# Two of the weight sums of a fast matrix product move from VectorE to accumulating DMAs, and fewer tiles are computed the classical way

## The chip, the core and the metric

The program runs on one core of one Trainium2 chip. The metric is the device time of one execution in microseconds (us), from the first to the last instruction of the core and the little that lies around it. Three runs of the kernel before gave 2911.69, 2925.96 and 2928.84 us; their median is 2925.96 us.

## The reference, cut to what matters

Two transformer blocks over 512 tokens of width 1024, all in float32. Around the change stand five feed-forward layers. Four of them (two in each of the two layers of the first block) are a gated product, the fifth has a convolution of width 3 over the tokens between the product and the gate:

```python
def swiglu(x, w_in, w_out):
    gate, up = jnp.split(x @ w_in, 2, axis=-1)
    return (jax.nn.silu(gate) * up) @ w_out

def conv_ffn(h, w_up, conv_w, conv_b, w_down):
    u = h @ w_up
    u = conv3(u, conv_w) + conv_b
    gate, val = u[..., :2816], u[..., 2816:]
    return (gelu(gate) * val) @ w_down
```

`x @ w_in` is 512 x 1024 by 1024 x 5632: 22 tiles of 128 columns for the gate and 22 for the other half ("up"). The convolution and its bias act on each column of `u` by itself.

## The kernel before

Every float32 matrix is split into a rounded part and a rest (`split`: ScalarE rounds to `h`, VectorE forms `l = src - h`), and every product is three matmuls (`mm3`, lines 292 to 294): h by h, h by the other's l, l by the other's h. The third needs the rest of the weights, `wl`.

An ffn (`ffn` for the four gated ones, the phase `ffn2` for the one with the convolution) works in pairs: pair m is gate tile m and up tile 22 + m, whose weights are 128 x 1024 each. There are 22 pairs. A pair is computed in one of two ways:

- classical: each tile is 8 blocks of 128 rows by two halves of 256 tokens, three matmuls each (`proj_t_steps` at the start of an ffn, `tile_t` in between). That is 96 matmuls of 256 columns for a pair.
- fast (`fast_weights`, `fast_pair`): the pair of tiles, the two halves of the 1024 rows and the two halves of the tokens are a 2 x 2 by 2 x 2 block product, done with 7 products instead of 8. A product is 4 blocks by three matmuls, 12 matmuls of 256 columns; the pair is 84. `fast_weights` makes the seven weight operands: the two halves of w1 (`r1`), two sums in the tile `s`, two in the tile `z`, and the second half of w2 (in `r2`). Four sums of 128 x 512 are made by VectorE (lines 449, 450, 453, 454), then each operand is split. `fast_pair` runs the products 0 to 6 in order and adds their results on ScalarE and VectorE. Products 0 and 1 take r1, 2 and 3 take s, 4 and 5 take z, 6 takes r2.

The token operands of the products 2, 3, 4 and 6 are sums and splits too: `fast_parts` makes them, two steps of four subtractions and three splits on VectorE (tiles `two`, `ts`), at the start of an ffn, when the last tokens have been normalised and transposed.

`FIRST` (2) classical pairs start each ffn, from m = 0, and lie beside `fast_parts`. In the four gated ffns the other 20 pairs are fast. In ffn2 every third pair after that is classical (6 of 20), since VectorE has the convolution there: two multiply-adds of 128 x 511 for a gate tile and two for an up tile (lines 1595, 1596), and the product of the two halves (line 1608).

The helper `ahead` writes the code of `fast_weights` of pair m + 1 behind the products of pair m and before the rest of pair m (silu, or convolution and gate). A scheduler then orders the instructions of each engine; the orders shown below are its result. Every engine runs its own list in order. Loads go out on SyncE's queue (SP). GpSimd (POOL) does only inverse square roots, some loads of gains and a few operations of the token mixing. The buffers concerned: three for raw weights (`wr`), three of each split part (`ws`), seven shared ones of 4 KB per partition (`t4`), which hold s, z, `two`, and in ffn2 `top` and `low`, the results of a fast pair.

Of the kernel before, what the change touches and what calls it, by code (L numbers as in the profile page):

```python
# [9 lines left out]
F32 = mybir.dt.float32  # L10
# [3 lines left out]
AF = mybir.ActivationFunctionType  # L14
ALU = mybir.AluOpType
# [3 lines left out]
S, D, DFF, DEPTH = 512, 1024, 2816, 2  # L19
NT, P = 4, 128  # L20
# [159 lines left out]


LAG, EARLY, OTHERS, DELTA, SLIDING, MLSTM = 24, 1, 2, 1, 1.3, 1
FIRST = 2


class Kernel:
# [192 lines left out]
    def fast_parts(self, pool, ps, keep=False):  # L379


        nc = self.nc
        self.load_late()
        part = lambda x, q, a: x[:, 4 * q:4 * q + 4, 256 * a:256 * a + 256]
        both = lambda q, a: (part(self.xh, q, a), part(self.xl, q, a))
        raw = self.raw
        room = lambda i: pool.tile([P, 1088], F32R, tag=f"T{i}", name="ts")[:, 48:1072].rearrange(
            "p (k n) -> p k n", k=4)
        ts = [[room(2 * i + j) for j in range(2)] for i in range(3)]
        for t, (p0, p1) in enumerate(ps):  # L390
            cs = slice(t * P, (t + 1) * P)
            r0, r1 = raw[0][:, :, cs], raw[1][:, :, cs]
            two = self.t4.tile([P, 2, 4, P], F32, tag="t4", name="two")
            nc.vector.tensor_sub(two[:, 0], p0, r0)
            nc.vector.tensor_sub(two[:, 1], p1, two[:, 0])
            nc.vector.tensor_sub(r0, two[:, 1], r0)
            nc.vector.tensor_sub(r1, r1, two[:, 1])
# [32 lines left out]
    def fast_weights(self, w1, w2):  # L430


        nc = self.nc
        r1, r2 = [self.wr.tile([P, 2, 4, P], F32, tag="raw", name="raw") for _ in range(2)]
        for r, w in ((r1, w1), (r2, w2)):
            nc.sync.dma_start(r.rearrange("p a k n -> p (a k n)"), w.rearrange("p k n -> p (k n)"))
        sub = nc.vector.tensor_sub
        ws = []

        def block(src):  # L440
            h = self.ws.tile(list(src.shape), F32R, tag="wh", name="wh")
            l = self.ws.tile(list(src.shape), F32R, tag="wl", name="wl")
            for i in range(src.shape[1]):
                nc.scalar.copy(h[:, i], src[:, i])  # L444
                ws.append((h[:, i], l[:, i]))
            sub(l, src, h.bitcast(F32))  # L446
        block(r1)
        s = self.t4.tile([P, 2, 4, P], F32, tag="t4", name="s")
        nc.vector.tensor_add(s[:, 1], r2[:, 0], r2[:, 1])
        sub(s[:, 0], s[:, 1], r1[:, 0])  # L450
        block(s)
        z = self.t4.tile([P, 2, 4, P], F32, tag="t4", name="z")
        sub(z[:, 0], r1[:, 0], r2[:, 0])
        sub(z[:, 1], r1[:, 1], s[:, 0])
        block(z)
        block(r2[:, 1:2])
        return ws

    def fast_pair(self, ws, xb, top, low):
# [12 lines left out]
        a, b = slice(0, 256), slice(256, 512)  # L472
        prod(0, x, start=True)
        nc.scalar.copy(top[:, a], x)  # L474
        prod(1, y, start=True)
        nc.vector.tensor_add(top[:, a], y, top[:, a])
        prod(2, x)
        nc.scalar.copy(top[:, b], x)
        prod(3, z, start=True)
        nc.scalar.copy(low[:, b], z)  # L480
        prod(4, x)
        nc.scalar.copy(low[:, a], x)
        nc.vector.tensor_add(low[:, b], low[:, a], low[:, b])
# [155 lines left out]
    def ffn(self, l, f):  # L639
        nc, io = self.nc, self.io  # L640
        base = 8 * l + (0 if f == 1 else 4)
        with self.phase(f"ffn{l}{f}") as pool:
# [5 lines left out]
            w = io[f"f{f}i{l}"]  # L648
# [17 lines left out]
            def products(m, ws):  # L666
                G, low = g[m // 2][:, m % 2], self.t2.tile([P, S], F32, tag="t2", name="low")
                X = self.fast_pair(ws, xb, G, low)

                def rest():  # L670
                    nc.scalar.activation(G, G, AF.Silu)
                    nc.vector.tensor_mul(G[:, 0:256], X, G[:, 0:256])
                    nc.vector.tensor_mul(G[:, 256:512], low[:, 256:512], G[:, 256:512])
                return rest
            self.ahead([(lambda m=m: self.fast_weights(w[m], w[KF + m]), lambda ws, m=m: products(m, ws))
                        for m in range(FIRST, KF)])
# [668 lines left out]
    def block2(self):  # L1345
# [237 lines left out]
            self.proj_n8(lhs, io["w2o"], KD, self.add_x8, [b1, b2, b3, b0], room)  # L1583

        with self.phase("ffn2") as pool:
            cv = pool.tile([P, 4, 56], F32, name="cv")
            nc.sync.dma_start(cv[:, :, 0:44], io["cv2"].rearrange("p (j m) -> p j m", j=4))
            pairs = self.ffn_banks()
# [4 lines left out]
            def conv(c, p, m):  # L1593
                A.activation(c, p, AF.Identity, scale=cv[:, 1, m:m + 1], bias=cv[:, 3, m:m + 1])
                V.scalar_tensor_tensor(c[:, 1:], p[:, 0:S - 1], cv[:, 0, m:m + 1], c[:, 1:], ALU.mult, ALU.add)
                V.scalar_tensor_tensor(c[:, 0:S - 1], p[:, 1:], cv[:, 2, m:m + 1], c[:, 0:S - 1], ALU.mult, ALU.add)

            def gate(m):
                def take(p):
# [1 line left out]
                    A.activation(gm(m), gm(m), AF.Gelu_apprx_tanh)  # L1601
                return take

            def up(m):
                def take(p):
                    c = self.t2.tile([P, S], F32, tag="t2", name="cup")
                    conv(c, p, 22 + m)
                    V.tensor_mul(gm(m), c, gm(m))
                return take
            tiles = []  # L1610
            for m in range(KF):
# [3 lines left out]

            def products(m, ws):
                top, low = [self.t4.tile([P, S], F32, tag="t4", name=n) for n in ("top", "low")]
                X = self.fast_pair(ws, xb, top, low)
                A.copy(low[:, 0:256], X)

                def rest():
                    gate(m)(top)
                    up(m)(low)
                return rest
            todo = []
            for m in range(FIRST, KF):
                if (m - FIRST) % 3 == 2:
                    todo += [(lambda n=n: self.load_t(tiles[n][0]),
                              lambda w, n=n: self.tile_t(xs, w, tiles[n][1])) for n in (2 * m, 2 * m + 1)]
                else:  # L1630
# [38 lines left out]
```

## Time and profile before

| | |
|---|---|
| runs shown | 2911.69, 2925.96, 2928.84 us, median 2925.96 |
| the profiled execution | 2919.21 us |
| its span | 2917.4 us |
| PE busy | 2853.4 us, 98% |
| DVE busy | 1952.8 us, 67% |
| ACT busy | 1425.8 us, 49% |
| POOL busy | 141.6 us, 5% |
| moved by DMA | 250.94 MB, of it 10.90 MB on POOL's queue |

PE is TensorE, DVE VectorE, ACT ScalarE. The profile is of one execution, so durations and waits are taken from its trace, and a sum of them stands beside its 2919.21 us. The end of a matmul is modelled: one of 256 columns is shown as 276 ns, while the next starts after 113 ns. What a stretch of matmuls costs is therefore read from the starts, not from the busy time. The same holds on DVE: a subtraction of 128 x 512 is shown as 0.68 us and the next starts 0.60 us after it.

### The profile page before, as it was taken

What the parts mean: (1) busy time and instruction counts of PE and PEld (TensorE: products, weight loads), DVE (VectorE), ACT (ScalarE), POOL (GpSimd) and SP (SyncE); (2) the same over time, 40 slices, a digit from 0 to 9 for tenths busy, and PEclk for the clock granted to TensorE, in tenths of its full rate; (3) what the DMA queues carried; (4) which work ended last, traced back from release to release, by engine and by line L of the source; (5) the groups of instructions that cost most, each with busy time, mean ns of one, the idle gap of its engine ahead of it and who ended that gap; (6) DMA issues with size and microseconds to landing.
All of it is one profiled execution on the core that took longest, in us unless ns stands there. A gap on an engine that the chain in (4) does not pass through costs nothing. (4 is left out here: it accounts for less than half of the span.)

```text
span 2917.4 us, 47905 instructions
## 1 busy us (share of the span) xinstructions
PE 2853.4 (98%) x19288; PEld 2525.3 (87%) x19288; DVE 1952.8 (67%) x3464; ACT 1425.8 (49%) x2784; POOL 141.6 (5%) x169
## 2 busy tenths in 40 slices
PE   7999999999999999999999999999999999999999
PEld 7998888877999878999887887899987877799987
DVE  7884555756888357887345666788635766689853
ACT  5663443343666345555334343466535456566641
POOL 0000000101000000000000000100000220000000
PEclk9999999999999999999999999999999999999999
DMA  4333322002233333333322001233342210313332
GB/s 154 110 123 109 96 82 65 8 3 71 94 110 116 109 101 94 102 109 112 120 68 85 24 8 37 73 110 110 120 134 81 94 44 1 95 60 109 102 102 93
DMA packets 74542, 250.94 MB, mean 86 GB/s; under 512 B 8624, under 2 KB 10800, under 8 KB 74064
## 3 DMA queue, kind: packets, MB, share of 16 engines
q1 hardware_dynamic: 71376, 236.99, 26.0%
q0 software_dynamic: 2944, 10.90, 1.1%
q8 instruction: 151, 2.47, 0.3%
q14 instruction: 71, 0.58, 0.1%
HBM read 245.76 MB, written 2.10 MB: 85 GB/s over the span
## 5 line engine op out<-in xcount | busy, mean ns | idle before, releaser
L281 DVE TENSOR_TENSOR wl<-raw,wh 128x1024 fp32r<-128x1024 f32 (+2 forms) x218 | 259.2, 1193 | 398.5 <-ACT wh L280 396.6
L280 ACT CAST wh<-raw 128x1024 fp32r<-128x1024 f32 (+2 forms) x218 | 223.7, 1027 | 457.8 <-PE psone L294 303.3
L292 PE MATMUL psfast<-xh,wh 128*128 128x256 f32 x1448 | 402.5, 278 | 0.0
L294 PE MATMUL psfast<-xh,wl 128*128 128x256 f32 x1448 | 401.4, 277 | 0.0
L293 PE MATMUL psfast<-xl,wh 128*128 128x256 f32 x1448 | 401.4, 277 | 0.0
L292 PE MATMUL psfast<-ts,wh 128*128 128x256 f32 x1184 | 328.7, 278 | 0.5
L293 PE MATMUL psfast<-ts,wh 128*128 128x256 f32 x1184 | 328.0, 277 | 0.0
L294 PE MATMUL psfast<-ts,wl 128*128 128x256 f32 x1184 | 328.0, 277 | 0.0
L293 PE MATMUL psone<-wl,gs 128*128 128x512 f32 x720 | 281.0, 390 | 0.0
L294 PE MATMUL psone<-wh,gs 128*128 128x512 f32 x720 | 280.2, 389 | 0.0
L292 PE MATMUL psone<-wh,gs 128*128 128x512 f32 x720 | 278.4, 389 | 0.0
L293 PEld LDWEIGHTS psfast<-xl,wh 128*128 128x128 f32 x1448 | 273.2, 189 | 0.2
L292 PEld LDWEIGHTS psfast<-xh,wh 128*128 128x128 f32 x1448 | 271.9, 188 | 1.4
L294 PEld LDWEIGHTS psfast<-xh,wl 128*128 128x128 f32 x1448 | 271.8, 188 | 0.0
L444 ACT CAST wh<-raw 128x512 fp32r<-128x512 f32 x282 | 175.1, 622 | 153.1 <-PE psfast L293 150.5
L292 PEld LDWEIGHTS psfast<-ts,wh 128*128 128x128 f32 x1184 | 222.4, 188 | 1.5 <-ACT top L474 1.5
L293 PEld LDWEIGHTS psfast<-ts,wh 128*128 128x128 f32 x1184 | 223.3, 189 | 0.0
L292 PE MATMUL psmm<-xh,wh 128*128 128x256 f32 (+1 forms) x712 | 222.1, 314 | 0.6 <-ACT xh L280 0.4
L294 PEld LDWEIGHTS psfast<-ts,wl 128*128 128x128 f32 x1184 | 222.3, 188 | 0.0
L293 PE MATMUL psmm<-xl,wh 128*128 128x256 f32 (+1 forms) x712 | 220.9, 311 | 0.0
L294 PE MATMUL psmm<-xh,wl 128*128 128x256 f32 (+1 forms) x712 | 219.6, 309 | 0.0
L446 DVE TENSOR_TENSOR wl<-raw,wh 128x1024 fp32r<-128x1024 f32 (+1 forms) x188 | 179.0, 952 | 59.0 <-PE psfast L294 36.5
(545 smaller groups left out, 6512.0 us busy)
## 6 DMA issues: line engine op xcount, KB each, us to landing
raw<-f1i SPq DMA_DIRECT2D x88, 512.0 KB, 3.5
raw<-f2i SPq DMA_DIRECT2D x88, 512.0 KB, 3.5
raw<-f1o SPq DMA_DIRECT2D x44, 512.0 KB, 3.8
raw<-f2o SPq DMA_DIRECT2D x44, 512.0 KB, 3.9
raw<-w2u SPq DMA_DIRECT2D x44, 512.0 KB, 3.5
raw<-w2d SPq DMA_DIRECT2D x22, 512.0 KB, 3.7
gain<-gains POOLq DMA_DIRECT2D x19, 512.0 KB, 4.1
raw<-wr SPq DMA_DIRECT2D x16, 512.0 KB, 4.1
```

The lines of the kernel that those rows point to most:

```text
L280: self.rounded = self.nc.scalar.copy(h, src)
L281: self.nc.vector.tensor_sub(l, src, h.bitcast(F32))
L292: mm(out, a[0], b[0], start=start, stop=False, **kw)
L293: mm(out, a[0], b[1], start=False, stop=False, **kw)
L294: mm(out, a[1], b[0], start=False, stop=stop, **kw)
L444: nc.scalar.copy(h[:, i], src[:, i])
L446: sub(l, src, h.bitcast(F32))
```

## The change

Four things, in one step.

1. Two of the four weight sums are made by DMA. The second half of w2 and the first half of w1 are added to a loaded half of w2 by two accumulating DMAs, issued by POOL; SP loads that half of w2 twice more, into s and z. A DMA can add but not subtract, so signs move: all that belongs to the second row of the block product comes out negated, and the multiplication that follows it negates again (a `scalar_tensor_tensor` by -1.0 in the gated ffns, negated convolution weights `minus` in ffn2). VectorE keeps two sums for each pair.
2. `FIRST` becomes 1: one classical pair at the start of each ffn instead of two.
3. In ffn2 every fifth pair after that is classical instead of every third: 4 of 21 instead of 6 of 20.
4. In ffn2 two operations of a fast pair go from VectorE to POOL: the addition to `low` in `fast_pair` (`adder`, line 485 after), and the product of the two halves (line 1612 after).

```diff
-FIRST = 2
+FIRST = 1
...
     def fast_weights(self, w1, w2):
...
         r1, r2 = [self.wr.tile([P, 2, 4, P], F32, tag="raw", name="raw") for _ in range(2)]
-        for r, w in ((r1, w1), (r2, w2)):
-            nc.sync.dma_start(r.rearrange("p a k n -> p (a k n)"), w.rearrange("p k n -> p (k n)"))
+        s, z = [self.t4.tile([P, 2, 4, P], F32, tag="t4", name=n) for n in "sz"]
+        nc.sync.dma_start(flat(s[:, 1]), part(w2, 0))
+        nc.sync.dma_start(flat(z[:, 0]), part(w2, 0))
+        nc.sync.dma_start(r1.rearrange("p a k n -> p (a k n)"), flat(w1))
+        nc.sync.dma_start(flat(r2[:, 1]), part(w2, 1))
+        nc.gpsimd.dma_start(flat(s[:, 1]), part(w2, 1), accum_op=ALU.add)
+        nc.gpsimd.dma_start(flat(z[:, 0]), part(w1, 0), accum_op=ALU.add)
...
         block(r1)
-        s = self.t4.tile([P, 2, 4, P], F32, tag="t4", name="s")
-        nc.vector.tensor_add(s[:, 1], r2[:, 0], r2[:, 1])
-        sub(s[:, 0], s[:, 1], r1[:, 0])
+        nc.vector.tensor_add(s[:, 0], s[:, 1], r1[:, 0])
         block(s)
-        z = self.t4.tile([P, 2, 4, P], F32, tag="t4", name="z")
-        sub(z[:, 0], r1[:, 0], r2[:, 0])
-        sub(z[:, 1], r1[:, 1], s[:, 0])
+        nc.vector.tensor_add(z[:, 1], r1[:, 1], s[:, 0])
         block(z)
         block(r2[:, 1:2])
...
-        nc.vector.tensor_add(low[:, b], low[:, a], low[:, b])
+        (adder or nc.vector).tensor_tensor(low[:, b], low[:, a], low[:, b], ALU.add)
...
-                    nc.vector.tensor_mul(G[:, 0:256], X, G[:, 0:256])
-                    nc.vector.tensor_mul(G[:, 256:512], low[:, 256:512], G[:, 256:512])
+                    for p, h in ((X, G[:, 0:256]), (low[:, 256:512], G[:, 256:512])):
+                        nc.vector.scalar_tensor_tensor(h, p, -1.0, h, ALU.mult, ALU.mult)
...
-            def up(m):
+            def up(m, *cv_):
                 def take(p):
                     c = self.t2.tile([P, S], F32, tag="t2", name="cup")
-                    conv(c, p, 22 + m)
-                    V.tensor_mul(gm(m), c, gm(m))
+                    conv(c, p, 22 + m, *cv_)
+                    (G if cv_ else V).tensor_tensor(gm(m), c, gm(m), ALU.mult)
                 return take
...
-                X = self.fast_pair(ws, xb, top, low)
+                X = self.fast_pair(ws, xb, top, low, G)
...
-                    up(m)(low)
+                    up(m, minus)(low)
...
-                if (m - FIRST) % 3 == 2:
+                if (m - FIRST) % 5 == 4:
```

`fast_parts` has its four subtractions turned in sign to fit (lines 394 to 397 before, 394 and 396 after); their number and size are the same. Line numbers after: 438 to 441 are the loads, 442 and 443 the accumulating DMAs, 454 and 456 the two sums that are left (s and z), 452 the rest parts, 485 the addition to `low`, 487 the second addition to `top`, 1599 and 1600 the convolution, 1612 the product, 659 the product of the classical up tile.

In ffn2, from one fast pair to the next, this stood on VectorE (the rows run from the first-half weights of the next pair, `wl<-raw`, to those of its s and z; `top`, `low` and `cup` belong to the pair that ends):

```order
L446 TENSOR_TENSOR wl<-raw,wh 128x1024
L483 TENSOR_TENSOR low<-low 128x256
L485 TENSOR_TENSOR top<-psfast,top 128x256
L450 TENSOR_TENSOR s<-s,raw 128x512
L454 TENSOR_TENSOR z<-raw,s 128x512
L1595 SCALAR_TENSOR_TENSOR g<-top,cv,g 128x511
L446 TENSOR_TENSOR wl<-s,wh 128x1024
L446 TENSOR_TENSOR wl<-z,wh 128x1024
```

and this stands there now:

```order
L452 TENSOR_TENSOR wl<-raw,wh 128x1024
L487 TENSOR_TENSOR top<-psfast,top 128x256
L1599 SCALAR_TENSOR_TENSOR g<-top,cv,g 128x511
L1600 SCALAR_TENSOR_TENSOR g<-top,cv,g 128x511
L1599 SCALAR_TENSOR_TENSOR cup<-low,minus,cup 128x511
L454 TENSOR_TENSOR s<-s,raw 128x512
L1600 SCALAR_TENSOR_TENSOR cup<-low,minus,cup 128x511
L456 TENSOR_TENSOR z<-raw,s 128x512
L452 TENSOR_TENSOR wl<-s,wh 128x1024
L452 TENSOR_TENSOR wl<-z,wh 128x1024
```

Three multiply-adds of the convolution now stand ahead of the sum s of the next pair and a fourth ahead of z; before, one of them stood behind both.

On POOL in ffn2 nothing stood before. Now, from one fast pair to the next, there is this (`g<-cup,g` is the product of the pair before, `low<-low` the addition of the present pair, and the two DMAs are the accumulations for the pair that follows it):

```order
L1612 TENSOR_TENSOR g<-cup,g 128x512
L485 TENSOR_TENSOR low<-low 128x256
L442 DMA s<-w2u 128x512
L443 DMA z<-w2u 128x512
L1612 TENSOR_TENSOR g<-cup,g 128x512
```

The accumulations for a pair stand behind the addition to `low` of the pair before it.

At the start of the second ffn VectorE now has, from the last steps of `fast_parts` to the first weights of s (`g<-psmm,g` is the product of the one classical up tile, `xl<-raw` belongs to the token operand of product 5):

```order
L394 TENSOR_TENSOR two<-raw,pstr 128x512
L452 TENSOR_TENSOR wl<-raw,wh 128x1024
L396 SCALAR_TENSOR_TENSOR two<-two,pstr 128x512
L396 SCALAR_TENSOR_TENSOR raw<-two,raw 128x4x128
L396 SCALAR_TENSOR_TENSOR raw<-two,raw 128x4x128
L659 TENSOR_TENSOR g<-psmm,g 128x512
L281 TENSOR_TENSOR ts<-two,ts 128x4x128 x2
L281 TENSOR_TENSOR ts<-raw,ts 128x4x128
L454 TENSOR_TENSOR s<-s,raw 128x512
L281 TENSOR_TENSOR xl<-raw,xh 128x4x256
L452 TENSOR_TENSOR wl<-s,wh 128x1024
```

The order is much as it was; what has moved is the matmuls beside it: two classical pairs before, one now.

## Rows read from the trace of the kernel before

**Rows 1.** The page, part 1: busy us, share of the span, instructions of each engine.
```profile
PE 2853.4 (98%) x19288; PEld 2525.3 (87%) x19288; DVE 1952.8 (67%) x3464; ACT 1425.8 (49%) x2784; POOL 141.6 (5%) x169
```

**Rows 2.** Windows: stretch, its us, then PE, PEld, DVE, ACT, POOL busy (instructions), clock, DMA.
```profile
762.80:953.40 190.60, 190.60 (x1681) 190.42 (x1681) 165.17 (x260) 119.05 (x243) 0.57 (x1) 1.00 0.35 114
1167.20:1365.10 197.90, 197.90 (x1681) 197.78 (x1680) 165.14 (x259) 119.21 (x243) 0.57 (x1) 1.00 0.34 108
2589.10:2792.80 203.70, 203.22 (x1755) 201.42 (x1754) 183.53 (x262) 129.12 (x241) 0.00 (x0) 1.00 0.33 104
```

**Rows 3.** Tile psmm on PE in one classical pair of ffn2: durations ns, first and last start.
```profile
L294 PE MATMUL psmm<-xh,wl x32: 276/276/276, 2609.4 to 2619.9; 128*128 128x256 f32 x32
```

**Rows 4.** Tile psmm on PE at the start of each ffn: last start is the end.
```profile
L294 PE MATMUL psmm<-xh,wl x56: 276/276/562, 22.6 to 44.5; 128*128 128x256 f32 x48, 128*128 128x512 f32 x8
L294 PE MATMUL psmm<-xh,wl x56: 276/276/415, 738.9 to 762.6; 128*128 128x256 f32 x48, 128*128 128x512 f32 x8
L294 PE MATMUL psmm<-xh,wl x56: 276/281/398, 1143.2 to 1167.0; 128*128 128x256 f32 x48, 128*128 128x512 f32 x8
L294 PE MATMUL psmm<-xh,wl x56: 276/281/415, 1868.9 to 1893.0; 128*128 128x256 f32 x48, 128*128 128x512 f32 x8
L294 PE MATMUL psmm<-xh,wl x56: 276/281/415, 2565.3 to 2589.0; 128*128 128x256 f32 x48, 128*128 128x512 f32 x8
```

**Rows 5.** Timeline of DVE at the start of the second ffn: start, us, instruction.
```profile
743.15 1.22 DVE L281 TENSOR_TENSOR wl<-raw,wh 128x1024 fp32r<-128x1024 f32 x1
...
747.54 1.29 DVE L281 TENSOR_TENSOR xl<-pstr,xh 128x512 fp32r<-128x512 f32 x2
...
758.29 1.21 DVE L446 TENSOR_TENSOR wl<-raw,wh 128x1024 fp32r<-128x1024 f32 x1
759.43 0.68 DVE L450 TENSOR_TENSOR s<-s,raw 128x512 f32<-128x512 f32 x1
760.03 0.68 DVE L453 TENSOR_TENSOR z<-raw 128x512 f32<-128x512 f32 x1
...
761.24 1.21 DVE L446 TENSOR_TENSOR wl<-s,wh 128x1024 fp32r<-128x1024 f32 x1
```

**Rows 6.** Timelines of DVE: the last token's splits in the first, third and fifth ffn.
```profile
21.88 2.48 DVE L281 TENSOR_TENSOR xl<-pstr,xh 128x512 fp32r<-128x512 f32 x4
...
1152.43 1.28 DVE L281 TENSOR_TENSOR xl<-pstr,xh 128x512 fp32r<-128x512 f32 x2
...
2569.51 1.29 DVE L281 TENSOR_TENSOR xl<-pstr,xh 128x512 fp32r<-128x512 f32 x2 [0.21 <-ACT xh L280]
```

**Rows 7.** Timelines of PE, DVE and ACT in ffn2, one fast pair and its end.
```profile
2620.02 0.28 PE L292 MATMUL psfast<-xh,wh 128*128 128x256 f32 x1
...
2627.04 1.22 DVE L446 TENSOR_TENSOR wl<-raw,wh 128x1024 fp32r<-128x1024 f32 x1 [0.38 <-ACT wh L444]
...
2628.51 0.42 DVE L485 TENSOR_TENSOR top<-psfast,top 128x256 f32<-128x256 f32 x1
...
2630.17 0.74 DVE L1595 SCALAR_TENSOR_TENSOR g<-top,cv,g 128x511 f32<-128x511 f32 x1
2630.83 1.22 DVE L446 TENSOR_TENSOR wl<-s,wh 128x1024 fp32r<-128x1024 f32 x1
...
2627.02 0.37 ACT L482 COPY low<-psfast 128x256 f32<-128x256 f32 x1
...
2628.97 0.82 ACT L1594 ACTIVATE g<-top,cv 128x512 f32<-128x512 f32 x1
```

**Rows 8.** Groups by line on POOL (busy us, mean ns, idle before), and the page's DMA issues.
```profile
L276 POOL TENSOR_TENSOR xr<-xrs,mhalf 128x1 f32<-128x1 f32 x40 | 24.5, 614 | 134.4 <-DVE xrs L275 134.2
L258 POOL DMA_DIRECT2D gain<-gains x19 | 11.2, 589 | 766.3 <-DVE wl L446 739.8 <-PE psD L1310 24.0 <-PE psmm L1507 1.9
L931 POOL TENSOR_TENSOR reg<-reg,consts 128x512 f32<-128x512 f32 x8 | 10.2, 1271 | 2.4 <-DVE reg L928 2.4
...
gain<-gains POOLq DMA_DIRECT2D x19, 512.0 KB, 4.1
```

**Rows 9.** Timeline of POOL in the second ffn's start.
```profile
743.32 1.46 POOL L276 TENSOR_TENSOR xr<-xrs,mhalf 128x1 f32<-128x1 f32 x1 [2.25 <-DVE xrs L275]
```

More of the change, by code (lines that the diff above doesn't have):

```diff
@@ L393, in fast_parts @@
             two = self.t4.tile([P, 2, 4, P], F32, tag="t4", name="two")
[L394 to L397, printed above, removed]
+            nc.vector.tensor_sub(two[:, 0], r0, p0)
+            for out, a, b in ((two[:, 1], two[:, 0], p1), (r0, two[:, 1], r0), (r1, two[:, 1], r1)):
+                nc.vector.scalar_tensor_tensor(out, a, -1.0, b, ALU.mult, ALU.subtract)
             for (h, l), src in zip(ts, (two[:, 0], two[:, 1], r0)):
@@ L433, in fast_weights @@
         nc = self.nc
+        flat = lambda z: z.rearrange("p k n -> p (k n)")
+        part = lambda w, q: flat(w[:, 4 * q:4 * q + 4])
         r1, r2 = [self.wr.tile([P, 2, 4, P], F32, tag="raw", name="raw") for _ in range(2)]
-        for r, w in ((r1, w1), (r2, w2)):
-            nc.sync.dma_start(r.rearrange("p a k n -> p (a k n)"), w.rearrange("p k n -> p (k n)"))
-        sub = nc.vector.tensor_sub
+        s, z = [self.t4.tile([P, 2, 4, P], F32, tag="t4", name=n) for n in "sz"]
[5 more added lines that the diff above has]
+        nc.gpsimd.dma_start(flat(z[:, 0]), part(w1, 0), accum_op=ALU.add)
         ws = []
@@ L445, in block @@
                 ws.append((h[:, i], l[:, i]))
-            sub(l, src, h.bitcast(F32))
+            nc.vector.tensor_sub(l, src, h.bitcast(F32))
         block(r1)
-        s = self.t4.tile([P, 2, 4, P], F32, tag="t4", name="s")
-        nc.vector.tensor_add(s[:, 1], r2[:, 0], r2[:, 1])
-        sub(s[:, 0], s[:, 1], r1[:, 0])
+        nc.vector.tensor_add(s[:, 0], s[:, 1], r1[:, 0])
         block(s)
-        z = self.t4.tile([P, 2, 4, P], F32, tag="t4", name="z")
-        sub(z[:, 0], r1[:, 0], r2[:, 0])
-        sub(z[:, 1], r1[:, 1], s[:, 0])
+        nc.vector.tensor_add(z[:, 1], r1[:, 1], s[:, 0])
         block(z)
@@ L457, in fast_weights, with fast_pair @@
         return ws
-    def fast_pair(self, ws, xb, top, low):
+    def fast_pair(self, ws, xb, top, low, adder=None):
         nc = self.nc
@@ L1585, in block2 @@
         with self.phase("ffn2") as pool:
-            cv = pool.tile([P, 4, 56], F32, name="cv")
+            cv = pool.tile([P, 4, 48], F32, name="cv")
             nc.sync.dma_start(cv[:, :, 0:44], io["cv2"].rearrange("p (j m) -> p j m", j=4))
+            minus = pool.tile([P, 4, 56], F32, name="minus")
+            V.tensor_scalar(minus[:, 0:3, 0:44], cv[:, 0:3, 0:44], -1.0, None, ALU.mult)
             pairs = self.ffn_banks()
@@ L1591, in block2, with conv @@
             gm = lambda m: g[m // 2][:, m % 2]
[L1593 to L1596, printed above, removed]
+            def conv(c, p, m, cv_=cv):
+                A.activation(c, p, AF.Identity, scale=cv_[:, 1, m:m + 1], bias=cv[:, 3, m:m + 1])
+                V.scalar_tensor_tensor(c[:, 1:], p[:, 0:S - 1], cv_[:, 0, m:m + 1], c[:, 1:], ALU.mult, ALU.add)
+                V.scalar_tensor_tensor(c[:, 0:S - 1], p[:, 1:], cv_[:, 2, m:m + 1], c[:, 0:S - 1], ALU.mult, ALU.add)
             def gate(m):
```

## The prediction, made before the result

> **What bounds the kernel now.** I read the page first. PE is busy for 98% of the span and no other engine for more than 67% [rows 1], so the kernel is bound by matmuls, as an average. Since busy PE is modelled, I then took the windows of the stretches that the change touches. Twenty fast pairs of the second ffn are 1680 matmuls in 190.6 us [rows 2]: 0.1135 us each, 9.53 us a pair, with nothing idle between them. DVE is busy 165 of those 190.6 us (instructions that overlap are counted once), so it keeps up without much slack. The third ffn has the same instructions and takes 197.9 us; the clock column says 1.00 there too, so I take those 7.3 us as scatter of this execution, which the change can't be held to. In ffn2, 14 fast and 6 classical pairs take 203.7 us [rows 2]. A classical pair there has 32 groups of three matmuls, the first and the last 10.5 us apart [rows 3]: 0.339 us a group, 10.85 us a pair. 14 x 9.53 + 6 x 10.85 = 198.5, so about 5 us of ffn2 are small waits.
>
> The gain that can be had from the matmuls is thus small: a fast pair is 1.3 us shorter than a classical one. What decides is whether a pair's weights are ready when PE comes to them. For that I read the timelines of DVE, ACT and POOL at the start of an ffn and inside ffn2.
>
> **Part 1: fewer classical pairs.** One pair in each ffn and two more in ffn2 change kind: 5 + 2 = 7 pairs x 1.32 = 9.2 us less PE work.
>
> **Part 2: the sums by DMA, gated ffns.** DVE loses two steps of 0.60 us for each pair (the pitch of rows 759.43 and 760.03 in [rows 5]). PE has no wait there to lose [rows 2], so this is worth 0 beyond the start. Two accumulations a pair land on POOL's queue, which is otherwise empty there; the buffers let s and z run some three pairs ahead, about 28 us, against 4.1 us for a load on that queue [rows 8]. I cost them at 0. If that cover is gone, every pair pays (a rival).
>
> **Part 3: the start of an ffn.** Before, two classical pairs (21.7 us of matmuls) lay beside the last token's splits, `fast_parts` and the first weights. Now one does. I count DVE's list forward from the last token's splits, at 0.60 us for 128 x 512 and 1.14 us for 128 x 1024 (758.29 to 759.43 in [rows 5]). Second ffn: those splits end at about 749.0 (in the trace 747.54 + 1.2; one step of `fast_parts` now stands ahead of them). Up to the end of `wl<-s` come 12 steps of 0.60 and 3 of 1.14: 749.0 + 7.2 + 3.4 = 759.6. PE has done its classical pair by about 752.5 and products 0 and 1 (2.7 us) by 755.4; product 2 needs `wl<-s` at its third matmul, so it starts at 759.4. Five products of 1.36 us later, at 766.2, pairs 0 and 1 are done. Before, they were done at 762.7 [rows 4]. So this start is 3.5 us longer, the saved matmuls included. The fourth ffn has the same order: 3.5.
>
> The same count elsewhere: the first ffn from 24.3 [rows 6]: 15 short and 4 long steps (one of them the second classical tile's weights) end at 37.9, with ACT's hand-overs some 38.5; done at 45.1 against 44.6 [rows 4], +0.6. The third ffn from 1153.6 [rows 6]: 10 short, one addition of 0.34 and 2 long steps, 1162.2; with 1.41 us a product there (197.9 / 140) done at 1169.1 against 1167.1, +2.0. ffn2 from 2570.7 [rows 6]: 15 short, 3 multiply-adds of 0.66 and 2 long ones give 2584.0; done at 2590.6 against 2589.1, +1.5. Sum of the five starts: +11.1 us. Bounds: if all of it hides, 5 x -1.3 = -6.6; if the first accumulation is late as well, some 4 us more each, +30.
>
> **Part 4: from one fast pair to the next in ffn2.** After the change m = 1 to 4, 6 to 9, 11 to 14, 16 to 19 and 21 are fast: 12 places where a fast pair follows a fast one. Take T = the start of product 5; in the pair that starts at 2620.02 that is 2626.8 [rows 7]. The next pair's product 2 stands four products later, at T + 5.4, and needs its `wl<-s` by T + 5.65.
> - ACT copies `low` at T + 0.2 to 0.6 [rows 7]. POOL's addition then reads two SBUF tiles. DVE is in `wl<-raw` from T + 0.2 to T + 1.4 [rows 7]. An instruction of POOL that began beside such a `wl` took 1.46 us [rows 9, 5], where the mean is 0.61 [rows 8]; it seems to be held until DVE's ends. So the addition runs from T + 1.4 for 0.65 us (half of 1.27 for 128 x 512 [rows 8]).
> - The accumulation of s is issued at T + 2.05. No accumulating DMA is in the trace. The nearest row is POOL's gain load, 4.1 us for twice the bytes [rows 8]; I take it, T + 6.15.
> - DVE: the second addition to `top` at T + 1.7 [rows 7]; ACT's part of the convolution ends at T + 2.97 [rows 7]; three multiply-adds of 0.66 (2630.17 to 2630.83 in [rows 7]) end at T + 5.0. The sum s waits for the DMA: T + 6.25 to 6.85. Then a multiply-add, z, and `wl<-s`: 0.66 + 0.60 + 1.14, T + 9.25.
> - PE waits 9.25 - 5.65 = 3.6 us at each of 12 places, 43 us. The next accumulation hangs on the next addition to `low`, which has moved by as much, so the wait comes again each time.
>
> Bounds of this wait: with the DMA in time, DVE's own order still ends at T + 8.0, 2.3 us. If POOL's product (1.27 us, free to start when the multiply-add ends) gets in ahead of `wl<-s`, it is 4.9.
>
> The Trainium skill (SBUF — State Buffer, "SBUF: two separate sides") says that a GpSimd instruction that reads SBUF and a VectorE one with two SBUF inputs exclude each other for a whole instruction; by that rule, which the 1.46 us bear out for POOL's side, the product would also hold up VectorE and the upper bound would be the likely one.
>
> The Trainium skill (DMA: Bandwidth & Descriptors, "Anatomy of one DMA — SWDGE (gpsimd) path") gives 2.0 us plus the bytes over 436 GB/s, an estimated 2.6 us for an accumulation if it cost what a load does; the trace's 4.1 us for 512 KB against 3.2 by that formula speaks for more, and by the formula the wait would be the lower bound.
>
> After pair 1, ffn2 is 16 fast and 4 classical pairs: 16 x 9.53 + 4 x 10.85 + 43 = 239 us; of the 5 us of small waits I keep half, 241.5 against 203.7: +37.8.
>
> **The sum.** 2919.2 + 11.1 + 37.8 = 2968 us, for the profiled execution. That one lies 6.8 us below the median of the runs shown, inside their spread of 17 us, so I leave the number as it is. A measurement of this kernel can tell about 1% from no change, 29 us: under 2897 is faster, over 2955 slower.
>
> **The rivals.**
> - *Matmuls decide everywhere, faster.* If the scheduler's order leaves room that I don't see (the weights of s ready by T + 5.65, `fast_parts` covered), only the 9.2 us less of PE and the 5 us of small waits go: 2905. For it: PE has no wait in any gated ffn [rows 2]. Against it: DVE's list alone ends at T + 8.0. It decides where `wl<-s` ends before T + 5.65.
> - *Half of it.* The accumulation lands early and the starts hide most: 12 x 2.3 = 28 and some 3 for the starts, less 7: 2943.
> - *POOL and DVE shut each other out.* The product goes ahead of `wl<-s`: 12 x 4.9 = 59 instead of 43, 2984. For it: the 1.46 us [rows 9]. Against: only POOL is seen to wait.
> - *The accumulations are slow everywhere.* If two of them take longer than a pair, each of about 100 fast pairs waits; at 1 us each, some 3060. Against: POOL's loads take 4.1 us, and DMA is busy a third of the time in these stretches [rows 2].
>
> **How the numbers follow.** My forecast 0.52 (2955 to 2980 by the bounds of parts 3 and 4), the faster rival 0.10, half of it 0.20, shut out 0.13, slow accumulations 0.05. Leaving out the last and most of the faster rival gives 2915 to 2996. Slower by over 1%: 0.48 of the forecast, 0.13, 0.05 and a little of "half", 0.68. Faster by over 1% is a corner of the faster rival, 0.04. Within 1%: the rest, 0.28.
>
> **What would show it.** In the new trace: fast pairs of the gated ffns still 9.5 us, without waits. In ffn2, a PE gap of 2.3 to 4.9 us at product 2 of 12 pairs and none behind a classical pair; ahead of it, the sum s on DVE waiting for a DMA that POOL issued after its addition to `low`. At the starts of the second and fourth ffn a gap of some 4 us ahead of product 2. I am wrong if ffn2's fast pairs follow each other at 9.5 to 10 us, or if s is waited for in the gated ffns.

## The result and the profile after

| | before | after |
|---|---|---|
| median of 4 runs | 2919.06 us (2911.69 to 2928.84) | 3060.82 us (3048.88 to 3062.42) |
| span of the profiled execution | 2917.4 us | 3047.1 us |

The ratio is 1.049, 95% interval 1.0464 to 1.0516: slower by 4.9%. I had said slower, and with 2968 us (range up to 2996) far too little. The page's first line answers to [rows 1]; the two others are its part 3, the DMA queues (packets, MB, share of 16 engines' span), q0 being POOL's.

```profile
PE 2902.0 (95%) x19324; PEld 2562.5 (84%) x19324; DVE 1873.3 (61%) x3296; ACT 1449.0 (48%) x2850; POOL 358.3 (12%) x405
...
q1 hardware_dynamic: 100464, 263.48, 28.0%
q0 software_dynamic: 32032, 63.86, 11.7%
```

VectorE lost 80 us of work, as was meant. PE's share fell by 3 points, so PE now waits. Its waits (total us, times, longest) by what ended them:

```profile
PE psfast L294 <- DVE wl L452: 31.4, 16, 2.3
PE psfast L292 <- ACT wh L450: 25.4, 29, 3.6
...
PE psfast L292 <- ACT g L476: 18.1, 32, 1.3
```

All three are waits of fast products. The windows say in which ffn; they are the stretch behind the first fast pair of the second, third and fifth ffn, and answer to [rows 2]:

```profile
780.60:984.40 203.80, 197.40 (x1682) 194.29 (x1681) 142.60 (x223) 117.71 (x244) 30.84 (x36) 1.00 0.71 176
1204.30:1404.40 200.10, 198.03 (x1682) 196.61 (x1682) 142.72 (x223) 118.90 (x244) 30.85 (x36) 1.00 0.72 178
2645.90:2922.00 276.10, 231.32 (x1730) 223.79 (x1729) 185.63 (x224) 143.25 (x265) 68.70 (x63) 0.89 0.49 122
```

PE is idle in ffn2 for 45 us and in a gated ffn for 2 to 6; the DMA engines' share in a gated ffn rose from 0.34 to 0.71; and ffn2's clock is 0.89.

For a budget I took the starts of all matmuls into `psmm` and `psfast` from each trace. *Start* is the time from an ffn's first `psmm` matmul to the first matmul of pair 2. Behind it, an interval of over 0.16 us counts as *wait*, less the 0.1135 us that a matmul takes; what the shorter ones have over 0.1135 is *pace*. Sums, in us:

| | before | after | difference |
|---|---|---|---|
| start, five ffns | 128.1 | 150.3 | +22.2 |
| wait, four gated ffns | 0.7 | 31.0 | +30.3 |
| wait, ffn2 | 3.2 | 77.8 | +74.6 |
| pace, five ffns | 7.9 | 15.4 | +7.5 |
| two more classical pairs of ffn2 fast | | | -2.6 |
| sum, against 129.7 between the spans | | | +132.0 |

The rest, -2.3, lies outside the ffns.

**One place of ffn2.** A fast pair starts at 2744.74, and product 5 of the pair ahead at T = 2741.9. The timeline, SP, POOL, DVE and then PE:

```profile
2738.86 0.38 SPq L438 DMA_DIRECT2D s<-w2u  x1
...
2742.57 1.28 POOL L485 TENSOR_TENSOR low<-low 128x256 f32<-128x256 f32 x1 [7.01 <-ACT low L484]
2743.78 0.87 POOL L442 DMA_DIRECT2D s<-w2u  x1
...
2749.44 1.57 POOL L1612 TENSOR_TENSOR g<-cup,g 128x512 f32<-128x512 f32 x1 [3.89 <-ACT wh L450]
...
2742.03 1.23 DVE L452 TENSOR_TENSOR wl<-raw,wh 128x1024 fp32r<-128x1024 f32 x1 [3.31 <-ACT wh L450]
...
2747.94 0.69 DVE L454 TENSOR_TENSOR s<-s,raw 128x512 f32<-128x512 f32 x1 [0.86 <-DMA s<-w2u]
...
2749.21 0.69 DVE L456 TENSOR_TENSOR z<-raw,s 128x512 f32<-128x512 f32 x1
2749.81 2.29 DVE L452 TENSOR_TENSOR wl<-s,wh 128x1024 fp32r<-128x1024 f32 x1
...
2752.15 0.38 PE L294 MATMUL psfast<-ts,wl 128*128 128x256 f32 x1 [2.25 <-DVE wl L452]
```

POOL's addition stands beside DVE's `wl<-raw` and takes 1.28 us; the accumulation is issued behind it, at T + 1.9, and the sum s starts as it lands, T + 6.0. Then POOL's product starts just ahead of `wl<-s`, which takes 2.29 us in place of 1.2, and PE gets it at T + 10.2. Behind this stop the matmuls are slow. The windows of this place, ahead of it and behind it (the clock is the third column from the right):

```profile
2744.74:2746.16 1.42, 1.42 (x15) 1.42 (x14) 1.29 (x2) 1.20 (x3) 0.81 (x1) 1.00 0.51 53
...
2753.18:2755.57 2.39, 2.39 (x14) 2.39 (x13) 0.99 (x3) 0.37 (x1) 0.00 (x0) 0.54 0.27 38
```

After a product with 3.4 us of stops the granted clock is down from 2.4 GHz to about 1.2, and matmuls follow each other at 0.213 us until 2756.8. In ffn2, 236 matmuls have that pitch: 23.8 of the 77.8 us. Stops proper are 53.5.

**One place of a gated ffn.** The second ffn, a pair that starts at 852.03: SP, POOL, DVE, ACT, PE.

```profile
847.58 0.33 SPq L440 DMA_DIRECT2D raw<-f2i  x1
...
847.95 0.86 POOL L442 DMA_DIRECT2D s<-f2i  x1 [7.83 <-DVE wl L452]
...
850.62 0.42 DVE L485 TENSOR_TENSOR low<-low 128x256 f32<-128x256 f32 x1
852.42 0.69 DVE L454 TENSOR_TENSOR s<-s,raw 128x512 f32<-128x512 f32 x1 [1.38 <-DMA raw<-f2i]
853.03 0.42 DVE L487 TENSOR_TENSOR g<-psfast,g 128x256 f32<-128x256 f32 x1
...
853.48 0.63 ACT L673 ACTIVATE g<-g 128x512 f32<-128x512 f32 x1 [1.59 <-DVE g L487]
...
855.05 0.36 ACT L476 COPY g<-psfast 128x256 f32<-128x256 f32 x1
...
855.47 0.39 PE L292 MATMUL psfast<-ts,wh 128*128 128x256 f32 x1 [0.55 <-ACT g L476]
```

Here the accumulations are in good time: the accumulation for the s that DVE adds at 852.42 went out at 837.73, a pair earlier, and the one shown is for the pair that follows. What is late is a plain load: r1, issued 0.4 us ahead of an accumulation, lands 4.8 us later. It could not go out sooner, since a raw buffer came free only at 847.55, with the end of a `wl<-raw` of 128 x 512 (846.86 + 0.69). DVE's sum s, which belongs to a later pair, stands in DVE's order right behind the addition to `low`, 3.5 us after r1's issue, and waits there for r1, ahead of the evacuation L487 of this pair; ACT and PE follow. So two things make this wait: the landing of r1 and the place of its reader.

### The profile page after: what moved, and what is told of

Same layout as the page of the kernel before. It is cut to its first block, busy times and chain, and to the rows that moved or that the text cites. A ratio compares the mean times of both kernels' runs of the same rounds, so it can differ in the third digit from the quotient of the medians.

```text
span 3047.1 us, 48947 instructions
## 1 busy us (share of the span) xinstructions
PE 2902.0 (95%) x19324; PEld 2562.5 (84%) x19324; DVE 1873.3 (61%) x3296; ACT 1449.0 (48%) x2850; POOL 358.3 (12%) x405
## 4 chain that ended last, share of the span: by engine, by line
PE 78%; DVE 9%; issue 4%; DMA 4%; ACT 3%; POOL 2%; SPq 0%; POOLq 0%; ACTq 0%; DVEq 0%
PE psfast L292 10%; PE psfast L294 9%; PE psfast L293 9%; PE psone L293 8%; PE psone L294 8%; PE psone L292 8%; DMA s<-w2u 2%; PE psmm L292 2%; PE psmm L293 2%; PE psmm L294 2%; PE pspn L292 2%; PE pspn L294 2%; PE pspn L293 2%; PE psO L1535 1%; DVE xn L322 1%
## 5 line engine op out<-in xcount | busy, mean ns | idle before, releaser
L292 PE MATMUL psfast<-xh,wh 128*128 128x256 f32 x1548 | 433.4, 280 | 0.1
L293 PE MATMUL psfast<-xl,wh 128*128 128x256 f32 x1548 | 431.1, 279 | 0.0
L292 PE MATMUL psfast<-ts,wh 128*128 128x256 f32 x1280 | 377.6, 295 | 48.2 <-ACT wh L450 25.4
L294 PE MATMUL psfast<-ts,wl 128*128 128x256 f32 x1280 | 370.2, 292 | 29.5 <-DVE wl L452 29.5
L293 PE MATMUL psfast<-ts,wh 128*128 128x256 f32 x1280 | 369.0, 288 | 0.0
L452 DVE TENSOR_TENSOR wl<-raw,wh 128x1024 fp32r<-128x1024 f32 x202 | 192.9, 955 | 196.7 <-ACT wh L450 195.5
L292 PEld LDWEIGHTS psfast<-ts,wh 128*128 128x128 f32 x1280 | 255.0, 199 | 62.8 <-ACT wh L450 31.3
L294 PEld LDWEIGHTS psfast<-ts,wl 128*128 128x128 f32 x1280 | 254.7, 200 | 32.8 <-DVE wl L452 32.8
L293 PEld LDWEIGHTS psfast<-ts,wh 128*128 128x128 f32 x1280 | 254.3, 199 | 0.0
L450 ACT CAST wh<-s 128x512 fp32r<-128x512 f32 x202 | 117.2, 618 | 105.0 <-PE psfast L293 71.9
L292 PE MATMUL psmm<-xh,wh 128*128 128x256 f32 (+1 forms) x528 | 165.9, 317 | 0.7 <-ACT xh L280 0.7
L293 PE MATMUL psmm<-xl,wh 128*128 128x256 f32 (+1 forms) x528 | 164.6, 313 | 0.8 <-DVE xl L281 0.8
```

The source lines that it names most:

```text
L292: mm(out, a[0], b[0], start=start, stop=False, **kw)
L293: mm(out, a[0], b[1], start=False, stop=False, **kw)
L294: mm(out, a[1], b[0], start=False, stop=stop, **kw)
L452: nc.vector.tensor_sub(l, src, h.bitcast(F32))
```

## The experiments

Each kernel ran 4 to 6 times against the kernel before on the same chip. The columns besides the time are those of the budget, from each kernel's profile. The change, e2 and e3 have the same gated ffns and show 31.0, 40.5 and 46.5 us of wait there, so a difference of less than some 15 us in that column tells nothing.

The scheduler orders every kernel anew, and an edit can move more than it says. At the 12 places of ffn2 three multiply-adds of the convolution stand ahead of the sum s on DVE in the change, e2, e3, f2, f3, f5, g1 and g4, none in e1, f1 and g2, and g3 has an order of its own. In the gated ffns the sum that reads r1 stands right behind the addition to `low` in the change, f1, f2 and all that keep two second transfers; in the kernel before, e1, g2 and g3 it stands behind `wl<-z` and `wl<-raw`. Runs of one order can be compared for what a transfer costs; across orders a difference holds both.

| kernel | us, median | ratio to before, interval | start | wait gated | wait ffn2 |
|---|---|---|---|---|---|
| before | | | 128.1 | 0.7 | 3.2 |
| the change | 3060.82 | 1.049 [1.0464, 1.0516] | 150.3 | 31.0 | 77.8 |
| e1 sums on VectorE | 2953.74 | 1.0127 [1.0073, 1.0182] | 149.2 | 1.0 | 19.9 |
| e2 addition, product on VectorE | 3048.35 | 1.045 [1.0409, 1.049] | 149.7 | 40.5 | 68.0 |
| e3 product on VectorE | 3053.5 | 1.0468 [1.0426, 1.051] | 146.5 | 46.5 | 69.0 |
| e4 before, FIRST = 1 | 2946.65 | 1.0091 [1.0056, 1.0125] | 146.7 | 0.6 | 3.4 |
| f1 no accumulation | 2954.15 | 1.0129 [1.0076, 1.0183] | 137.3 | 4.6 | 10.1 |
| f2 plain second load | 3016.26 | 1.0335 [1.0285, 1.0384] | 145.4 | 8.1 | 63.3 |
| f3 first loads on POOL | 3056.94 | 1.048 [1.0423, 1.0538] | 146.1 | 38.7 | 76.9 |
| f5 the change, FIRST = 2 | 3043.42 | 1.0444 [1.0386, 1.0502] | 128.4 | 54.0 | 79.1 |
| g1 e2 and f3 together | 3020.91 | 1.0384 [1.036, 1.0407] | 145.4 | 45.6 | 35.0 |
| g2 e1, FIRST = 2 | 2926.28 | 1.0054 [1.0039, 1.0069] | 128.2 | 0.8 | 18.9 |
| g3 only z accumulated | 2992.89 | 1.0299 [1.0254, 1.0344] | 146.3 | 0.6 | 43.8 |
| g4 raw loads first | 3063.04 | 1.0527 [1.0506, 1.0548] | 147.7 | 43.8 | 80.2 |

**e1: the sums back on VectorE.**

```diff
-        nc.gpsimd.dma_start(flat(s[:, 1]), part(w2, 1), accum_op=ALU.add)
-        nc.gpsimd.dma_start(flat(z[:, 0]), part(w1, 0), accum_op=ALU.add)
+        nc.vector.tensor_add(s[:, 1], r2[:, 0], r2[:, 1])
+        nc.vector.tensor_add(z[:, 0], r1[:, 0], r2[:, 0])
```

> The changed kernel with the two sums made by VectorE again (both rows of weights loaded whole, no accumulating DMA); one classical pair at the start, the addition to low and the product in ffn2 on POOL as in the change. Theory A (the accumulating loads put waits into every fast pair of the gated ffns, and the longer part of the wait in ffn2): the four gated ffns lose their 10 to 10.8 us pairs and come back to 9.5 us, some 40 us less; ffn2's 12 places fall from 6.6 us of wait to about 3 (VectorE's own order and POOL's operations stay), some 40 us less: 2970 to 2985 us. Theory B (the waits come from the negated row and POOL's operations, the accumulations are covered): the gated ffns keep their 10 to 10.8 us pairs and the time stays over 3040.

It came out under theory A's range: 107 us less than the change, the gated waits gone, ffn2's down by 58. Without the accumulating loads, and with the order that VectorE has without them, about three quarters of the loss are gone. With the DMA out of the way, 12 places of ffn2 still cost 19.9 us, 1.7 each; PE then waits for something else:

```profile
PE psfast L292 <- ACT top L474: 14.0, 11, 1.6
```

**e2 and e3: POOL's operations back on VectorE.**

```diff
-                    (G if cv_ else V).tensor_tensor(gm(m), c, gm(m), ALU.mult)
+                    V.tensor_tensor(gm(m), c, gm(m), ALU.mult)
...
-                X = self.fast_pair(ws, xb, top, low, G)
+                X = self.fast_pair(ws, xb, top, low)
```

e2 has both hunks, e3 the first alone.

> The changed kernel with ffn2's addition to low and its product back on VectorE; the accumulating loads stay. Theory A (POOL's addition, which VectorE shuts out, holds the next accumulation back, and POOL's product holds VectorE's weights up): accumulations in ffn2 are issued some pairs ahead, as in the gated ffns, and ffn2's fast pairs come down from 16.2 to between 10 and 11.5 us: 12 x 5 = 60 us less, about 3000; the gated ffns unchanged. Theory B (the accumulation itself is what is late in ffn2, whoever adds): the pairs stay over 15 us and the time over 3045.

> The changed kernel with only the product of ffn2 back on VectorE; the addition to low stays on POOL. Theory A1 (most of the difference between my 3.6 us and the 6.6 us of the trace is POOL's product shutting VectorE out for 1.1 us, and a slow TensorE clock behind the longer wait): the weights of s take 1.2 us again; if VectorE's product stands behind them the 12 places lose 1 to 2.5 us each, 3030 to 3048; if it stands ahead of them, they gain what they lose, 3055 to 3065. Theory A2 (the queue behind the addition decides alone): no difference, within 5 us of the changed kernel.

Theory A of e2 fell: 12 us less instead of 60. The time that theory B forecast came (over 3045), but g1 below shows that its reason, the accumulation itself, is not the whole of it. In e3 VectorE's product stands behind `wl<-s` and ffn2's wait fell by 8.8 us, less than A1 had; the time lies between A1's cases, because the gated ffns of this execution waited more. That POOL's product holds DVE is true all the same: the group of `wl<-s` in ffn2 has a mean of 2015 ns in the change and of 1218 in e3 (the first row is the change's, the second e3's).

```profile
L452 DVE TENSOR_TENSOR wl<-s,wh 128x1024 fp32r<-128x1024 f32 x16 | 32.2, 2015 | 0.0
```

```profile
L452 DVE TENSOR_TENSOR wl<-s,wh 128x1024 fp32r<-128x1024 f32 x16 | 19.5, 1218 | 0.0
```

That is 16 x 0.797 = 12.8 us of DVE's time. Why e2 gave no more shows in its timeline:

```profile
2744.30 0.33 SPq L419 DMA_DIRECT2D raw<-w2u  x1
2744.72 0.38 SPq L438 DMA_DIRECT2D s<-w2u  x1
...
2749.04 0.86 POOL L442 DMA_DIRECT2D s<-w2u  x1 [13.27 <-DVE top L487]
...
2743.54 0.69 DVE L452 TENSOR_TENSOR wl<-raw,wh 128x512 fp32r<-128x512 f32 x1
...
2753.04 0.69 DVE L454 TENSOR_TENSOR s<-s,raw 128x512 f32<-128x512 f32 x1 [1.11 <-DMA s<-w2u]
```

The *first* load of s, on SP, is late now. It stands in SP's order behind a raw load, which has to wait until `wl<-raw` of the pair ahead lets its buffer go (2743.54 + 0.69). Load and accumulation in series then take 2744.72 to 2753.04, 8.3 us; the load lands at 2748.5, and the profile gives as the end of POOL's wait DVE's L487, which ended at 2748.84, so 0.4 us of the 8.3 may be that. In the change that load goes out at 2738.86, a moment after the same release (`wl<-raw`, 2737.70 + 0.68); with 3.8 us, the median of these loads in ffn2, it lands at 2742.7, and POOL's addition is done at 2743.85. Two holds of nearly one length, of which I had seen one.

**e4: the kernel before with one classical pair at the start.**

```diff
-FIRST = 2
+FIRST = 1
```

> The kernel before with one classical pair at the start of each ffn in place of two, and nothing else (no negated row, no accumulations). In ffn2 the place of the classical pairs among the fast ones shifts by one. My count of the starts gave +11 us with the accumulations and the extra steps of the change; without them VectorE has the two sums in its list and one step less in the third ffn: +8 to +14 over the kernel before. If the longer starts of the changed kernel come from the accumulations alone, the time is 5 to 7 us under the kernel before (five classical pairs became fast ones at 1.3 us each).

18.6 us in the starts (in ffn2 seven of 21 pairs are classical here, so four pairs became fast ones, not five), and in this execution pace of 6.5 more than in the profile before; the ratio is 0.9%, with the median beyond the range that I gave.

**f1 and f2: no second transfer, and a plain one.**

```diff
-        nc.gpsimd.dma_start(flat(s[:, 1]), part(w2, 1), accum_op=ALU.add)
+        nc.gpsimd.dma_start(flat(s[:, 1]), part(w2, 1))
```

That is f2, with the same for z; f1 drops both lines.

> The changed kernel without its two accumulating loads; the plain loads of s and z on SP stay, and everything else. It leaves the addition of the second half out, so s and z hold one half only. Theory C (in ffn2 and in the gated ffns the second transfer comes in series behind the first, and each fast pair waits for the chain of two): the gated ffns come back to 9.5 to 9.9 us a pair, ffn2's places to 10.5 to 12 us, in all 2950 to 2970. Theory D (what is late is the first plain load, which stands in SP's order behind loads that wait for raw buffers, whatever follows it): ffn2's places stay over 13 us and the gated ffns over 10; over 3010.

> The changed kernel with plain loads in place of the two accumulating loads, on the same queue, of the same bytes to the same tiles and in the same order behind the first loads; it leaves the addition out, so s and z hold the second half only. Theory C1 (a second transfer in series is what costs, and it costs the same whether it adds or not): within 15 us of the changed kernel, gated pairs of 10 to 10.8 us. Theory C2 (the adding itself is dear: it reads the tile as well and holds the DMA engines, so that raw loads land later): gated pairs 9.5 to 9.9, ffn2's places 2 us shorter, 2990 to 3015.

f1: the times of theory C, D falls. In the gated ffns f1 has the change's order, and r1 lands in 4.2 us. In ffn2 the sum s stands ahead of the convolution here, so the 10.1 us there are not the price of the missing transfer alone. (Some 20 us of f1's profile lie between the first and the second ffn, where this execution had a granted clock of 0.84; its stages are compared, not its total.) f2, with the change's order in both, splits the loss: ffn2 keeps 63.3 of the 77.8 us with a plain second transfer (C1's number), while the gated ffns keep 8.1 of 31.0 (C2); the time is a shade beyond C2's range. The 63.3 us are mostly no wait for a transfer, though: at s DVE waits for a DMA 8.8 us in all of ffn2, 13.5 in the change. DMA in 800 to 960 us, the change and then f2 (packets, MB, share of 16 engines; below, count, KB, us to landing):

```profile
q0 software_dynamic: 4635, 8.51, 31.4%
...
raw<-f2i SPq DMA_DIRECT2D x15, 512.0 KB, 4.7
...
s<-f2i POOLq DMA_DIRECT2D x15, 256.0 KB, 5.6
```

```profile
q0 software_dynamic: 2544, 8.39, 14.5%
...
raw<-f2i SPq DMA_DIRECT2D x15, 512.0 KB, 4.2
...
s<-f2i POOLq DMA_DIRECT2D x15, 256.0 KB, 4.3
```

For the same bytes, adding takes 2.2 times the engines' time (31.4 against 14.5), and r1 lands 0.5 us later. With sums on VectorE it lands in 3.5 us; the step from there to f1's 4.2 comes without any second transfer.

**f3 and g1: the first loads away from SP's order.**

```diff
-        nc.sync.dma_start(flat(s[:, 1]), part(w2, 0))
-        nc.sync.dma_start(flat(z[:, 0]), part(w2, 0))
+        nc.gpsimd.dma_start(flat(s[:, 1]), part(w2, 0))
+        nc.gpsimd.dma_start(flat(z[:, 0]), part(w2, 0))
```

g1 has e2's two hunks besides.

> The changed kernel with the plain loads of s and z issued on POOL's queue in place of SP's, ahead of the accumulations; what is computed is the same. Theory D (SP's order holds these loads back behind loads that wait for raw buffers): ffn2's places lose 1 to 4 us each, gated pairs come to 9.5 to 10 us as raw loads no longer stand behind them, 2980 to 3030. Theory C (the chain of two transfers and the load of the DMA engines): POOL's queue now stands still while it waits for the load that it accumulates on, so s of the pair is accumulated before z's load is issued or the other way about: no gain, 3045 to 3090.

> The changed kernel with ffn2's addition and product on VectorE and, besides, the plain loads of s and z on POOL's queue: neither SP's order (behind loads that wait for raw buffers) nor a computing instruction of POOL stands ahead of a load or an accumulation any more. Theory F (in ffn2 two holds of the same length coincide, SP's order for the first load and POOL's addition for the second, so that taking one away gave 6 to 12 us): PE's waits in ffn2 behind pair 1 fall from 68 to 78 us to 20 to 40 us, 2995 to 3020. Theory C (two transfers in series are late in ffn2 wherever they are queued, for want of buffers): the waits stay over 60 us and the time over 3040.

f3 alone gives nothing (C of its expectations), e2 alone 10 us of ffn2's wait, both together 43 of 78: theory F, inside its range for ffn2, and by 1 us beyond it in time. What is left in g1 shows on POOL and DVE at one place, and in PE's waits there:

```profile
2737.90 0.92 POOL L442 DMA_DIRECT2D s<-w2u  x1
...
2748.76 0.75 DVE L1599 SCALAR_TENSOR_TENSOR cup<-low,minus,cup 128x511 f32<-128x511 f32 x1
2749.42 0.69 DVE L454 TENSOR_TENSOR s<-s,raw 128x512 f32<-128x512 f32 x1
...
2751.28 1.22 DVE L452 TENSOR_TENSOR wl<-s,wh 128x1024 fp32r<-128x1024 f32 x1
```

```profile
PE psfast L294 <- DVE wl L452: 14.4, 12, 1.2
```

The accumulation goes out a pair ahead and has long landed (4.5 us, the median in ffn2) when DVE comes to s, and in all of ffn2 DVE waits for no DMA. What PE still waits for is DVE's own order: s starts as the third multiply-add of the convolution lets DVE go. These stops are 25.7 us, 2.1 a place; slow matmuls behind them make up most of the rest of the 35.0. The change adds to this DVE's wait for the accumulated s, 13.5 us by the row below (busy us, mean ns, idle before), and POOL's product, 12.8: together 52 us, next to its 53.5 of stops. No run changes the order alone.

```profile
L454 DVE TENSOR_TENSOR s<-s,raw 128x512 f32<-128x512 f32 x16 | 11.0, 690 | 13.5 <-DMA s<-w2u 13.5
```

**f5 and g2: two classical pairs at the start again**, by FIRST = 2 in the change and in e1.

> The changed kernel with two classical pairs at the start of each ffn again (FIRST = 2), everything else as in the change. One classical pair more costs 1.3 us of matmuls in each ffn, and the place of ffn2's classical pairs shifts by one (15 or 16 fast pairs, 12 places). If the start prices add to the rest as in the kernel before (20 to 36 us for five ffns with FIRST = 1 alone): 3020 to 3040. If the waits behind the start are what decides and the longer start only gives the accumulations room: within 8 us of the changed kernel.

> The changed kernel with the two sums on VectorE (no accumulating load) and two classical pairs at the start of each ffn; left of the change are the negated row, POOL's addition and product in ffn2 and one classical pair in five there. If prices add: the kernel with VectorE's sums less the start's price of 20 to 36 us, so 2918 to 2934, within 1% of the kernel before, with ffn2 still some 10 us longer than before and nothing lost in the gated ffns. If one classical pair in five were a gain by itself, under 2905.

Both starts fall to what they were before, 128.4 and 128.2. f5 is 17 us under the change, between its two theories: the starts gave 22, and the gated waits of this execution are the largest of all. g2 is additive: 0.5% above the kernel before, nothing lost in the gated ffns, and 15.7 us of waits in ffn2, for two fewer classical pairs and POOL's two operations together. No version beat the kernel before.

**g3 and g4: one accumulation; the raw loads first.** g3 loads r2 whole and makes s on VectorE, z by load and accumulation; g4 moves the two raw loads ahead of those of s and z.

```diff
-        nc.sync.dma_start(flat(s[:, 1]), part(w2, 0))
-        nc.gpsimd.dma_start(flat(s[:, 1]), part(w2, 1), accum_op=ALU.add)
+        nc.vector.tensor_add(s[:, 1], r2[:, 0], r2[:, 1])
```

> The changed kernel with one accumulating load for each fast pair: z still comes by load and accumulation, the sum s is made by VectorE from both halves, loaded whole. Theory E (in the gated ffns what costs is the time that accumulations hold the DMA engines, so that raw loads land late): PE's waits behind pair 1 of the four gated ffns fall from 31 us to 3 to 12 us. Theory C (any accumulation in the chain is late): they stay over 20 us. For ffn2, where the weights of s are needed first, no second transfer stands ahead of s any more: its waits fall from 78 us to 20 to 40 us if the chain through s is the cause, and stay over 60 if z's chain would be as late. In all 2965 to 3000 by E and the chain through s; over 3030 otherwise.

> The changed kernel with the loads of the raw rows issued ahead of those of s and z, on the same queue. Theory G (in the gated ffns a raw load is late because it stands in SP's order behind the loads of s and z, which wait for their buffers): PE's waits in the four gated ffns fall from 31 us to under 15 us. Theory E (raw loads land late because the accumulations hold the DMA engines): they change by less than 10 us. In ffn2 the loads of s and z stand behind both raw loads, so its waits stay or grow by up to 12 us: 3030 to 3045 by G, 3050 to 3070 by E.

With one accumulation a pair the gated waits are 0.6 us, better than E asked; with the order changed they are 43.8, within the scatter of that column, and G falls. DMA of g3, same stretch:

```profile
q0 software_dynamic: 2308, 4.46, 16.1%
...
raw<-f2i SPq DMA_DIRECT2D x30, 512.0 KB, 4.2
```

The 4.2 us are the median of r1 and r2 together. By themselves r1 lands in 4.6 us, hardly sooner than in the change (4.7), and r2 in 3.6. That PE does not wait is due to DVE's order: the sum that reads r1 comes 9.8 us after its issue (844.28 to 854.06 in one pair), against 3.5 in the change. So E's number came, but g3 does not bear out its reason: raw loads are late here too, and it costs nothing. f1 and f2, with the change's order, do. G could not help: in the change r1's load waits for a raw buffer itself (SP waits for `wl<-raw` ahead of it 19 times in the second ffn), whoever stands ahead of it. ffn2 keeps 43.8 us, just above the range: the longest wait there is now 4.4 us, ended by ACT's copy of `top` (L475). How much of that is z's chain, how much POOL's two operations and how much the order, these runs don't separate.

## Why the prediction was wrong

- *Part 1, fewer matmuls, -9.2.* Nothing speaks against it; it is inside the starts and ffn2, and no run shows it alone.
- *Part 2, accumulations in the gated ffns at 0.* This step failed: 30 us in the profile after, up to 46 in runs with the same code there. The accumulations are early, as I said, and the wait of a whole pair that my rival feared is not there. I asked when they land and not what they do to others, nor where DVE's new order puts the readers of plain loads: they hold the DMA engines 2.2 times as long as plain loads of their bytes, r1's landing went from 3.5 to 4.7 us (0.5 of it by the adding, as f2's 4.2 shows), and r1's reader stands 3.5 us behind r1's issue and ahead of an evacuation. It takes both. f1 and f2 keep the order, r1 lands in 4.2 us and the waits are 4.6 and 8.1; g3 has r1 land in 4.6 us and its reader late, and the wait is 0.6. The accumulations with the order before, or a fourth raw buffer, were not tried.
- *Part 3, starts, +11.1.* Measured +22.2. By ffn I had 0.6, 3.5, 2.0, 3.5 and 1.5, and it was 4.9, 4.1, 6.0, 3.7 and 3.6: the second and fourth came out, and the miss lies in the other three. f1, without sums of either kind, has +9.2, near my sum, but by ffn 1.5, 1.5, 1.7, 1.5 and 3.1, so that nearness is luck. That the accumulations would be there in time failed: they cost 13 us, no less than VectorE's sums (e1, e4). The bound (+30) held.
- *Part 4, ffn2's 12 places, 3.6 us each.* Every link is in the trace: the addition held by `wl<-raw` (1.28 us), the accumulation issued at T + 1.9 (2.05 said), s at T + 6.0 (6.15). Two sizes failed. My sum left POOL's product out, and it goes in ahead of `wl<-s`: T + 10.2 for T + 9.25, so my upper bound (4.9) was the better one; stops proper are 53.5 us, 4.5 a place. The rule of the Trainium skill (SBUF — State Buffer, "SBUF: two separate sides") had said so, and 2015 against 1218 ns agrees. And a stop drops the clock: 2 us a place more, which I had at nothing. In all 77.8 where I had 43.
- *What hides behind the link.* I named POOL's addition as what holds the accumulation. That was one of two: e2 shows the first load's place on SP, g1 that only both together matter. The bound "DMA in time", 2.3, is the case of g1, 2.1 a place; e1's 1.7 is of another order and no test of it. So about half of the stops is DVE's order, which I had counted rightly.
- *The rivals.* Shut out was right as a mechanism and far from the whole. "Slow everywhere, some 3060" met the number for another reason: 0.4 us a gated pair (31 us over 80), not 1, and most of the loss in ffn2. "Matmuls decide" and "half of it" fell.
- The Trainium skill's price of a DMA (DMA: Bandwidth & Descriptors, "Anatomy of one DMA — SWDGE (gpsimd) path") gave an estimate of 2.6 us for an accumulation. Runs show 4.1 for s in ffn2 and 5.6 in a gated ffn; my 4.1 for ffn2 came out, but by luck: I took it from a gain load of twice the bytes, and a plain load of 256 KB on that queue lands in 3.0 us in ffn2 (f2).

Sum by these steps: 11 + 38 said; 22 + 30 + 72 + 7 of pace measured.

## What to carry to other kernels

A transfer that adds is not free because its queue is empty: add up the time for which it holds the DMA engines, and ask which plain load is then late, how soon its reader comes and who stands behind that reader. The same late landing cost 31 us in one order of VectorE (the change) and nothing in another (g3). An edit that takes a transfer away can move that order too, so look at it before you give the transfer the difference. A load with an accumulation on it is two transfers in series, 8 us here, so it needs both queues and its buffer free that much sooner; if two queues hold it for the same time, freeing one shows nothing. Price a stop of PE with the slow matmuls that follow it.

## What the hardware showed that I had not expected

- An accumulating load holds the DMA engines 2.2 times as long as a plain one of its bytes, and it is cut finer: 4635 packets for 8.51 MB on POOL's queue against 2544 for 8.39 MB in f2, a gain load of 0.52 MB among both.
- Matmuls have a second pace at a granted clock of 1.00: in the kernel before 885 in 100 us of the second ffn and 851 in the third, 0.1135 and 0.1177 us apart. Some ffns of an execution have it and others in the next, up to 7 us each; in the predicted sum I had taken it for scatter, and that stands, but what sets it stayed open.

```profile
800.00:900.00 100.00, 100.00 (x885) 100.00 (x884) 86.80 (x137) 62.04 (x127) 0.00 (x0) 1.00 0.34 111
...
1180.00:1280.00 100.00, 100.00 (x851) 100.00 (x851) 83.93 (x134) 59.31 (x121) 0.00 (x0) 1.00 0.32 106
```
